# RG-LRU from its input projection on, layer 1's input normalised first, S5's powers in one tile

## The chip, the cores and the metric

The kernel runs on one core of a Trainium2 chip. The time is device time of one execution in microseconds; the time before is 1248.59 us, the median of three runs (1243.89 to 1249.86).

## The reference

Two layers of a hybrid decoder trunk on x of 512 tokens by 1024 channels, float32. Each layer computes

```
h = RMSNorm(x, ln_mix_pre);  p = h @ w_in          # columns go to four mixers of 256 channels
m = concat[GLA(p_A), DiffAttn(p_B), S5(p_C), RG-LRU(p_D)] @ w_out
x = x + RMSNorm(m, ln_mix_post)
x = x + RMSNorm(relu(RMSNorm(x, ln_ffn_pre) @ ffn_w1)**2 @ ffn_w2, ln_ffn_post)

RMSNorm(x, g) = x * rsqrt(mean(x*x) + 1e-6) * g    # per token
RG-LRU: xc = conv4(rx); r, i = sigmoid(xc @ w_a + b_a), sigmoid(xc @ w_x + b_x)
        a = exp(-8 r softplus(-lam)); h_t = a h_(t-1) + sqrt(1 - a^2) (i * xc); out = h * gelu(rg)
S5:     a complex diagonal state per group of 16 channels; its tables need the powers w^0 .. w^127
        of each state's rotation, as cosine and sine
GLA:    gate = log_sigmoid(glr @ w_gate + b_gate) / 16, glr being a projection of rank 16
```

## The kernel before

"Layer 1" is the first layer (l = 0 in the code), "layer 2" the second.

Activations lie with channels on the partitions, 512 tokens along a row. Every float32 product of a weight W and an input X is made of three matmuls on split operands: high parts h and wh, rounded to the TensorE format, and remainders l and wl (`mm3`, L294: wh h, wh l, wl h). A weight of 4x128 rows by 256 columns is loaded into one of three `raw` buffers (L256), cast to wh by ScalarE and subtracted to wl by VectorE or GpSimd (`w_part`, L245; which of the two is `E.split_eng`, where 'g' is GpSimd). For layer 2 the split weights have been stored in DRAM ahead (`early_gen`).

The instructions are written as generators. A projection yields between its pieces, and at each yield the mixers that run in the background are advanced by given rates (`advance`, L1139). The program order so made gives each instruction its priority; a scheduler then puts each engine's queue in order at build time, and each engine works through its queue in that order. `tc.high_priority(offset=O.evp)` raises an instruction's priority; the evictions of the projections' accumulators out of PSUM have it. BANKS gives projections two banks each of `pg` and three of `pd`.

Start of layer 1 (L1192 to L1239). TensorE runs WARM = 38 matmuls on zeros. x is loaded transposed (`xT`), slice by slice of 128 channels with quarters of the first four weights between them; each slice is scaled by the norm's gain alone and split into h and l (L1225). So the first projection, dqk (queries and keys of the attention, `gemm_first`, L330), starts before the norm's token scale is known. Squares of the slices are added up (`SumSq`), TensorE sums them over channels (L541), VectorE makes the reciprocal root (`rkeep`, L1239) and TensorE spreads it over the partitions (L548) into `rbc`. Every eviction of layer 1's projections then multiplies by `rbc` on VectorE (L1340, L1359, L1392), the rotary tables do so too (L1327), and the token-major ones scale on ScalarE (L1374).

All later norms work otherwise: squares with a running sum per block of 128 tokens (L1280), a root (L1260), the identity times that scale (`dg`, L1286), and `make` (L1288): TensorE multiplies x by `dg`, which transposes and scales it at once, ScalarE writes h (L1302) and VectorE l (L1303), two blocks of tokens at a time. `gemm_blocks` (L353) then runs the product for the first 256 tokens, calls the second `make`, and runs the second half.

Order of the projections in layer 1: dqk, dv, glr, gqk, gv, gog, u, rg, rx; in layer 2 the last are rx, rg. `glr_gen` (L1378) makes the gate's input of rank 16; its copy out of PSUM (L1392) has ordinary priority. `maybe_start` (L1400) starts a mixer when its inputs are projected: the attention (`diff_gen`, L1046; scores L1063, exponentials L1078, transposes L1098) after dqk and dv, S5 after u, RG-LRU after rx and rg both. S5's preparation (`s5_prep_gen`, L608) runs behind dqk in layer 1 and beside layer 1's feed-forward for layer 2; its last part makes the powers: for each half of the channels seven doublings of the tables COS and SIN, six VectorE instructions each (`cmul`, L669). `lru_gen` (L850) convolves rx (L858, L861), multiplies by the gates' weights (L867, L868), makes a and the input of the recurrence, scans (L895), and multiplies by the GELU of rg (L899, L901). The output projection (`gemm_wide`, L408) takes the mixers' results in the order GLA, attention, S5, RG-LRU.

Of the kernel before, what the change touches and what calls it, by code (L numbers as in the profile page):

```python
# [17 lines left out]
P = 128  # L18
# [94 lines left out]
def host_pack(I):  # L113
# [31 lines left out]
    return dict(xT=np.ascontiguousarray(I["x"][0].T), xt=np.ascontiguousarray(I["x"][0]),  # L145
# [25 lines left out]
def hybrid_trunk(ctx, tc, I, out, consts):  # L171
# [158 lines left out]
    def gemm_first(wids, xs, consume):  # L330

        ps = [(pd if m // 2 % 2 else pg)() for m in range(4)]
        for kh in range(2):
            W = [w_get(w[kh]) for w in wids]

            def prod(m, k):
                cs = slice(m % 2 * P, m % 2 * P + P)
                Wm, kk = W[m // 2], 4 * kh + k
                mm3(ps[m], Wm[0][:, k, cs], Wm[1][:, k, cs], xs[kk][0], xs[kk][1], kk == 0, kk == 7)

            for k in range(2 if kh else 4):
                for m in range(4):
                    prod(m, k)
                yield
            if kh:
                for m in range(4):
                    for k in (2, 3):
                        prod(m, k)
                    with tc.high_priority(offset=O.evp):
                        consume(m, ps[m])  # L350
                    yield

# [159 lines left out]

    class SumSq:

        def __init__(self, eng, tail):
            self.acc, self.eng, self.tail = None, eng, tail
            self.ends = {}

        def add(self, c, src, hf=None):
            if hf is None:
                sq = wq("sq")
                act.activation(sq, src, AF.Square)
                if c >= self.tail:
                    self.ends[c] = sq
                elif self.acc is None:
                    self.acc = sq
                else:
                    self.eng.tensor_tensor(self.acc, self.acc, sq, ALU.add)  # L530
            else:
                if c not in self.ends:
                    self.ends[c] = wq("sq")
                act.activation(self.ends[c][:, 256 * hf:256 * hf + 256], src, AF.Square)

        def tok(self, bs=range(4)):
            ps = psm()
            tl = [self.acc] + list(self.ends.values())
            for b in bs:
                for i, t in enumerate(tl):  # L540
                    pe.matmul(ps[:, b:b + 1], t[:, b * P:b * P + P], C[:, C_BO + 6:C_BO + 7],  # L541
                              start=i == 0, stop=i == len(tl) - 1)
            return ps[:, bs[0]:bs[-1] + 1]

    def bcast_tok(col, n=4):
        ps = psm()
        for b in range(n):
            pe.matmul(ps[:, b * P:b * P + P], col[:, b:b + 1].to_broadcast([P, P]), ident,  # L548
                      start=True, stop=True)
        return ps[:, 0:n * P]  # L550
# [57 lines left out]
    def s5_prep_gen(l):  # L608
# [138 lines left out]
        yield  # L747
        for h in range(2):
            js = slice(4 * h, 4 * h + 4)
            tabs = [wt(k) for k in ("COS", "SIN", "RC")]  # L750
            ct, st, rc = (t.rearrange("p (j c) -> p j c", j=4) for t in tabs)
            pool.memset(ct[:, :, 0:1], 1.0)
            pool.memset(st[:, :, 0:1], 0.0)
            for e in range(7):
                m = 1 << e
                wr, wi = (w[:, 8 * e + 8:8 * e + 16] for w in (csw, snw))
                cmul(ct[:, :, m:2 * m], st[:, :, m:2 * m], ct[:, :, 0:m], st[:, :, 0:m],
                     bc(wr, m, js), bc(wi, m, js), 4, m)
# [91 lines left out]
    def lru_gen(l, xr, gt):  # L850
# [47 lines left out]
        for a in range(2):  # L898
            act.activation(gt[a], gt[a], AF.Gelu_apprx_tanh)  # L899
# [289 lines left out]
    sync.dma_start(PV, I["cols"])  # L1189
# [14 lines left out]
    if WARM:  # L1204
# [3 lines left out]
        act.copy(small(1, "zact", 1), z[:, 0:1])  # L1208
# [3 lines left out]
    setup_exp()  # L1212
    ssq = SumSq(v, 7)
    xin = []
    for c in range(8):
        w2 = (c // 4 * 2, c // 4 * 2 + 1)
        if c % 4 == 0:
            for i in w2:
                w_raw(i)
                w_open(i)  # L1220
        xin.append(wl("x"))
        sync.dma_start(xin[c], I["xT"][c * P:c * P + P, :])
        for i in w2:
            sync.dma_start(raws[i][:, c % 4], specs[i][:, c % 4])
        XG[c] = hl(xin[c], pv("ln_mix_pre", 0, 8, c))  # L1225
        for i, e in zip(w2, (v, pool)):
            w_part(i, slice(c % 4, c % 4 + 1), e)
        if c % 4 == 3:
            for i in w2:
                del raws[i]  # L1230
    pos[:] = [4, 4]
    sync.dma_start(C, consts[:, 0:C_N])
    w_load(3 + NRAW)
    for c in range(8):
        ssq.add(c, xin[c])
    ms = small(4, "ms4")
    v.tensor_scalar(ms, ssq.tok(), 1.0 / D, EPS, ALU.mult, ALU.add)
    rtok = small(4, "rkeep")
    v.tensor_copy(rtok, rsqrt(ms, 4))  # L1239

    def post_norm(grow, g2=None):
# [3 lines left out]
        ss, sx, part = small(8, "ss"), small(8, "sx"), small(4, "part")  # L1245
        gB = [wq("gB") for _ in range(2)]
        for c in range(2):
            sync.dma_start(gB[c], grow[:, c * 512:c * 512 + 512].to_broadcast([P, 512]))

            pool.tensor_scalar(gB[c], gB[c], 32.0, None, ALU.mult)  # L1250
        F, dg = {}, {}

        def stat(b, ct, o, f=None):
            act.activation(wq("sq"), o, AF.Square, accum_out=ss[:, 4 * ct + b:4 * ct + b + 1])
            F[b, ct] = o if f is None else f
            v.tensor_tensor(F[b, ct], o, gB[ct], ALU.mult)
            if ct == 0 and b == 3:
                v.tensor_scalar(part, ss[:, 0:4], D * EPS, None, ALU.add)

        def root(a, b):  # L1260

            y, t, xh = (small(1, k) for k in ("qy", "qt", "qh"))
            act.activation(t, a, AF.Sqrt, bias=b)
            v.tensor_scalar(xh, a, b, -0.5, ALU.add, ALU.mult)
            v.reciprocal(y, t)
            v.scalar_tensor_tensor(t, y, xh, y, ALU.mult, ALU.mult)
            v.scalar_tensor_tensor(y, t, 1.5, y, ALU.add, ALU.mult)
            return y

        def finish(b):  # L1270
            sc = root(ss[:, 4 + b:5 + b], part[:, b:b + 1])
            for c in range(2):
                if g2 is None:
                    o = wp.tile([P, 4, 256], F32, tag="raw", name=nm("o"), bufs=NRAW)
# [6 lines left out]
            if g2 is None:  # L1281
                return
# [275 lines left out]
```

## Time and profile before

| | before |
|---|---|
| median of three runs | 1248.59 us (1243.89 to 1249.86) |
| profiled execution, own time | 1246.94 us |
| its span, first to last instruction | 1244.9 us |
| mean granted TensorE clock | 0.976 |
| busy, share of the span: TensorE | 1201.6 us, 97% |
| VectorE | 683.9 us, 55% |
| ScalarE | 509.2 us, 41% |
| GpSimd | 194.2 us, 16% |

PE is TensorE's matmuls, PEld its weight loads, DVE VectorE, ACT ScalarE, POOL GpSimd, SP the queue that issues the DMAs. The profile names each instruction by the line of the kernel, here L followed by its number, and by the tiles that it writes and reads (out<-in). A granted clock of 1.00 is TensorE's full speed. Idle time of an engine is put down to the instruction that released it; a matmul's end is modelled, so starts are the better numbers.

### The profile page before, as it was taken

Reading aid. Unit: us, or ns where it says so; the run is one execution under the profiler, and the core shown is the slowest. Engines: PE = TensorE matmul, PEld = TensorE weight load, DVE = VectorE, ACT = ScalarE, POOL = GpSimd, SP = SyncE. Lnnn points to the kernel's source line nnn. Section 1 sums busy time; section 2 is a strip of 40 time slices with the busy share of each in tenths; the row PEclk is TensorE's granted clock in tenths of the full one; section 3 lists DMA queues with packets and bytes.
Section 4 is the critical chain, followed back from the end, with each engine's and each line's share of the span. In section 5 each row is a group of like instructions: output and inputs, shape, how many; then the busy total and the mean of one; then the engine's idle time right before and its main releaser. Section 6 shows DMA issues by size and latency. Waiting matters only on the chain.

```text
span 1244.9 us, 17841 instructions
## 1 busy us (share of the span) xinstructions
PE 1201.6 (97%) x6684; PEld 967.6 (78%) x6684; DVE 683.9 (55%) x1605; ACT 509.2 (41%) x950; POOL 194.2 (16%) x148
## 2 busy tenths in 40 slices
PE   8988899899999999999999999999999999999997
PEld 6755566579888888888889776777988888888886
DVE  8987568578725576545474256575641131322335
ACT  5253622456735523424341356145542341332332
POOL 5321212300000001000000000010123323333330
PEclk9998889999999999999999999899999999999999
DMA  7343122456867887866754432355432333333221
GB/s 229 98 141 116 35 86 82 136 168 208 265 211 235 283 292 241 267 210 212 253 195 141 155 109 91 116 198 203 170 100 88 100 102 92 100 97 101 87 83 67
DMA packets 126037, 191.81 MB, mean 154 GB/s; under 512 B 10688, under 2 KB 65792, under 8 KB 125952
## 3 DMA queue, kind: packets, MB, share of 16 engines
q1 hardware_dynamic: 125952, 190.69, 47.4%
q8 instruction: 52, 0.85, 0.3%
q14 instruction: 33, 0.27, 0.1%
HBM read 146.35 MB, written 44.30 MB: 153 GB/s over the span
## 4 chain that ended last, share of the span: by engine, by line
PE 83%; DVE 10%; ACT 3%; DMA 1%; issue 1%; SPq 0%; DVEq 0%; ACTq 0%
PE pg L295 7%; PE pg L296 7%; PE pg L297 7%; PE pd L296 5%; PE pd L297 5%; PE pd L295 5%; PE pd L415 4%; PE pd L417 4%; PE pd L416 4%; PE pg L415 4%; PE pg L417 3%; PE pg L416 3%; PE pd L1063 2%; PE pm L415 2%; PE pm L416 2%; PE pm L417 2%
## 5 line engine op out<-in xcount | busy, mean ns | idle before, releaser
L253 ACT CAST wh<-raw 128x1024 fp32r<-128x1024 f32 (+1 forms) x160 | 157.4, 985 | 257.4 <-PE pg L416 88.2
L254 POOL TENSOR_TENSOR wl<-raw,wh 128x1024 fp32r<-128x1024 f32 (+1 forms) x69 | 156.9, 2275 | 383.3 <-ACT wh L253 380.7
L295 PE MATMUL pg<-h,wh 128*128 128x512 f32 (+1 forms) x496 | 189.4, 383 | 2.6 <-DVE glr L1392 2.5
L297 PE MATMUL pg<-h,wl 128*128 128x512 f32 (+1 forms) x496 | 188.9, 382 | 0.2 <-DVE wl L254 0.2
L296 PE MATMUL pg<-l,wh 128*128 128x512 f32 (+1 forms) x496 | 188.4, 381 | 0.5 <-DVE l L479 0.5
L254 DVE TENSOR_TENSOR wl<-raw,wh 128x1024 fp32r<-128x1024 f32 (+1 forms) x91 | 105.9, 1164 | 144.2 <-ACT wh L253 144.0
L297 PE MATMUL pd<-h,wl 128*128 128x512 f32 (+1 forms) x336 | 120.7, 360 | 0.0
L295 PE MATMUL pd<-h,wh 128*128 128x512 f32 (+1 forms) x336 | 120.6, 360 | 0.0
L296 PE MATMUL pd<-l,wh 128*128 128x512 f32 (+1 forms) x336 | 120.4, 359 | 0.0
L295 PEld LDWEIGHTS pg<-h,wh 128*128 128x128 f32 x496 | 95.7, 193 | 21.7 <-DVE glr L1392 2.9
L297 PEld LDWEIGHTS pg<-h,wl 128*128 128x128 f32 x496 | 95.7, 193 | 17.6 <-issue 1.4
L296 PEld LDWEIGHTS pg<-l,wh 128*128 128x128 f32 x496 | 95.8, 193 | 17.0 <-DVE l L479 1.2
L1474 DVE TENSOR_TENSOR s<-r 128x512 f32<-128x512 f32 x64 | 56.7, 886 | 87.4 <-ACT r L1473 87.4
L415 PE MATMUL pd<-wh,h 128*128 128x512 f32 x240 | 93.7, 390 | 0.9 <-DMA wh<-early 0.9
L417 PE MATMUL pd<-wl,h 128*128 128x512 f32 x240 | 93.6, 390 | 0.4 <-DVE wl L254 0.4
L416 PE MATMUL pd<-wh,l 128*128 128x512 f32 x240 | 93.4, 389 | 0.0
L415 PE MATMUL pg<-wh,h 128*128 128x512 f32 x208 | 81.4, 391 | 1.4 <-ACT h L475 1.4
L416 PE MATMUL pg<-wh,l 128*128 128x512 f32 x208 | 81.0, 389 | 0.0
L417 PE MATMUL pg<-wl,h 128*128 128x512 f32 x208 | 81.0, 389 | 0.0
L297 PEld LDWEIGHTS pd<-h,wl 128*128 128x128 f32 x336 | 63.6, 189 | 9.4
L295 PEld LDWEIGHTS pd<-h,wh 128*128 128x128 f32 x336 | 63.2, 189 | 9.6 <-ACT wh L253 0.3
L296 PEld LDWEIGHTS pd<-l,wh 128*128 128x128 f32 x336 | 63.5, 189 | 9.4
(421 smaller groups left out, 2162.6 us busy)
## 6 DMA issues: line engine op xcount, KB each, us to landing
raw<-in_ffn_w SPq DMA_DIRECT2D x128, 512.0 KB, 3.9
early<-eh SPq DMA_DIRECT2D x52, 256.0 KB, 3.1
early<-el SPq DMA_DIRECT2D x52, 256.0 KB, 4.1
wh<-early SPq DMA_DIRECT2D x23, 512.0 KB, 3.6
wl<-early SPq DMA_DIRECT2D x23, 512.0 KB, 4.7
ex<-in_w_in SPq DMA_DIRECT2D x36, 256.0 KB, 4.8
raw<-in_w_in SPq DMA_DIRECT2D x14, 512.0 KB, 3.7
xd<-xr SPq DMA_DIRECT2D x24, 256.0 KB, 2.9
```

Source lines behind the costliest of these rows:

```text
L253: act.copy(h[:, k], raws[i][:, k])
L254: eng.tensor_tensor(lo[:, k], raws[i][:, k], h[:, k].bitcast(F32), ALU.subtract)
L295: pe.matmul(ps, wh, xh, start=first, stop=False, **kw)
L296: pe.matmul(ps, wh, xl, start=False, stop=False, **kw)
L297: pe.matmul(ps, wl, xh, start=False, stop=last, **kw)
L415: pe.matmul(o, xs[kk][0][:, ts_], h, start=kk == 0, stop=False)
L416: pe.matmul(o, xs[kk][1][:, ts_], h, start=False, stop=False)
L417: pe.matmul(o, xs[kk][0][:, ts_], lo, start=False, stop=kk == 7)
L1063: pe.matmul(pp[c], qs[h // 2][r:r + 32, i * P:i * P + P], ks[h // 2][r:r + 32, 0:pp[c].shape[1]], start=i == blocks[0], stop=False, tile_p ...
L1474: v.tensor_tensor(s, r, r, ALU.mult)
```

## The change

Layer 1's input goes through the same norm as all others: `post_norm` is cut in two, and its second part, `pre_norm`, is used at the start with x loaded token-major. `rbc`, `SumSq`, `bcast_tok` and `gemm_first` are gone; layer 1's evictions are plain ScalarE copies as in layer 2, and dqk runs through `gemm_blocks`. The first three weights are loaded whole, split on VectorE, into other slots of SBUF. The constants are loaded second, the small columns (PV) after block 1 of x. WARM is 80. `glr`'s copy gets the evictions' priority. Layer 1 projects rx before rg; in both layers RG-LRU starts when rx is there and waits for rg only before its last step. S5's first four doublings are made in one tile for both halves, with both parts of the complex number in one instruction, and copied into the tables by ScalarE.

```diff
@@ s5_prep_gen
+        pw = wq("pw")[:, 0:256].rearrange("p (c j m) -> p c j m", c=2, j=8)
+        pool.memset(pw[:, 0, :, 0:1], 1.0)
+        pool.memset(pw[:, 1, :, 0:1], 0.0)
+        for e in range(4):
+            m = 1 << e
+            wr, wi = (w[:, 8 * e + 8:8 * e + 16] for w in (csw, snw))
+            xa, xb = (wq("cm")[:, 0:16 * m].rearrange("p (c j m) -> p c j m", c=2, j=8) for _ in range(2))
+            tt(xa, pw[:, :, :, 0:m], bc2(wr, m), ALU.mult)
+            tt(xb, pw[:, :, :, 0:m], bc2(wi, m), ALU.mult)
+            tt(pw[:, 0, :, m:2 * m], xa[:, 0], xb[:, 1], ALU.subtract)
+            tt(pw[:, 1, :, m:2 * m], xa[:, 1], xb[:, 0], ALU.add)
+            yield
         for h in range(2):
...
-            pool.memset(ct[:, :, 0:1], 1.0)
-            pool.memset(st[:, :, 0:1], 0.0)
-            for e in range(7):
+            for c, t in enumerate((ct, st)):
+                act.copy(t[:, :, 0:16], pw[:, c, js])
+            for e in range(4, 7):
...
@@ lru_gen
         for a in range(2):
+            while gt[a] is None:
+                yield
             act.activation(gt[a], gt[a], AF.Gelu_apprx_tanh)
@@ the start
-        act.copy(small(1, "zact", 1), z[:, 0:1])
+        act.activation(small(1, "zact", 1), z[:, 0:1], AF.Sqrt)
...
-        sync.dma_start(xin[c], I["xT"][c * P:c * P + P, :])
-        for i in w2:
-            sync.dma_start(raws[i][:, c % 4], specs[i][:, c % 4])
-        XG[c] = hl(xin[c], pv("ln_mix_pre", 0, 8, c))
...
-    v.tensor_copy(rtok, rsqrt(ms, 4))
+    def pre_norm(g2, keep):
+        sx, dg = small(8, "sx"), {}
+        def half(b, c):
+            act.activation(wq("sq"), X[b, c], AF.Square, accum_out=sx[:, 2 * b + c:2 * b + c + 1])
+        def done(b):
             m0 = small(1, "ms2")
             v.tensor_scalar(m0, sx[:, 2 * b:2 * b + 1], D * EPS, None, ALU.add)
             dg[b] = small(P, "dg")
...
+            if keep:
+                for e in range(2):
+                    for c in range(2):
+                        spill(b + e, c)
+        return half, done, make
+    E.split_eng = "v"
+    half, done, make = pre_norm(lambda c: pv("ln_mix_pre", 0, 8, c), False)
+    x_load(0)
+    sync.dma_start(C, consts[:, 0:C_N])
+    x_load(1)
+    sync.dma_start(PV, I["cols"])
+    home.update(enumerate((wg, wg, wb)))
+    w_load(1)
+    x_load(2)
+    x_load(3)
+    w_load(2)
+    for b in range(4):
+        for c in range(2):
+            half(b, c)
+        done(b)
+        if b == 1:
+            make(0)
+            setup_exp()
@@ ev_mul (ev_silu and ev_tok likewise)
-                if l == 0:
-                    v.tensor_tensor(o, i, r, ALU.mult)
-                else:
-                    act.copy(o, i)
+                act.copy(o, i)
@@ glr_gen
-            if l == 0:
-                v.tensor_tensor(t, ps, rbc[0:32], ALU.mult)
-            else:
+            with tc.high_priority(offset=O.evp):
                 v.tensor_copy(t, ps)
@@ maybe_start
-            if "lru" not in started and have("rx", "rg"):
+            if "lru" not in started and have("rx"):
                 started.add("lru")
+                st["rg"] = [None, None]
                 start(lru_gen(l, st["rx"], st["rg"]), O.rate["lru"])
@@ the projections
-                g = gemm_first if l == 0 else lambda *a: gemm_blocks(*a, make)
-                g = g(WID[l, "dqk"], XG, lambda m, ps: evs[m // 2](m % 2, ps))
+                g = gemm_blocks(WID[l, "dqk"], XG, lambda m, ps: evs[m // 2](m % 2, ps), make)
@@ parameters
-WARM = 38
+WARM = 80
-    dict(order=["dqk", "dv", "glr", "gqk", "gv", "gog", "u", "rg", "rx"],
+    dict(order=["dqk", "dv", "glr", "gqk", "gv", "gog", "u", "rx", "rg"],
```

## Rows read from the trace of the kernel before

**Rows 1.** By stage: window, length, PE, PEld, DVE, ACT, POOL busy, clock, DMA, GB/s.

```profile
0.00:37.00 37.00, 32.26 (x163) 25.98 (x164) 33.49 (x138) 20.05 (x39) 17.71 (x22) 0.95 0.70 216
37.00:112.00 75.00, 62.50 (x427) 47.72 (x425) 70.53 (x288) 31.35 (x87) 22.38 (x23) 0.95 0.40 126
112.00:165.00 53.00, 49.54 (x186) 30.39 (x187) 31.08 (x91) 28.34 (x61) 9.53 (x8) 0.76 0.16 51
165.00:228.00 63.00, 57.09 (x627) 42.64 (x626) 44.86 (x98) 16.35 (x24) 14.39 (x13) 0.97 0.34 100
228.00:242.00 14.00, 10.74 (x30) 5.85 (x29) 11.07 (x13) 4.64 (x8) 6.12 (x3) 0.88 0.47 165
...
284.00:640.00 356.00, 355.86 (x1753) 299.24 (x1754) 209.52 (x398) 158.00 (x260) 8.06 (x16) 1.00 0.73 237
...
700.00:850.00 150.00, 147.73 (x1080) 105.50 (x1078) 88.58 (x235) 71.67 (x168) 7.37 (x13) 0.97 0.40 137
```

**Rows 2.** TensorE's waits, 0 to 285 us: who for whom; total, times, longest.

```profile
PE pd L1098 <- ACT p L1078: 5.1, 2, 3.9
PE pd L1063 <- ACT p L1078: 4.4, 2, 2.4
PE pd L867 <- DVE xc L861: 3.3, 1, 3.3
...
PE pg L295 <- DVE glr L1392: 2.5, 1, 2.5
```

**Rows 3.** Timeline of the start, TensorE: start, duration, line, operands, idle before.

```profile
0.97 4.11 PE L1211 MATMUL pm<-zero 128*128 128x128 bf16 x38 [0.97 <-DVE zero L1207]
...
36.66 0.28 PE L391 MATMUL pg<-wh,h 128*128 128x256 f32 x1
```

**Rows 4.** Timeline at the boundary of the two layers, 640 to 652 us.

```profile
641.07 0.29 ACT L1263 ACTIVATE qt<-ss,part 128x1 f32<-128x1 f32 x1
...
642.45 1.42 DVE L1279 SCALAR_TENSOR_TENSOR xr<-f,qy,xr 128x512 f32<-128x512 f32 x2
...
642.88 1.95 PE L1298 MATMUL pg<-dg,xr 128*128 128x128 f32 x16
...
643.24 0.63 ACT L1280 ACTIVATE sq<-xr 128x512 f32<-128x512 f32 x1 [1.87 <-DVE xr L1279]
...
644.91 0.46 ACT L1302 ACTIVATE h<-pg,PV 128x256 fp32r<-128x256 f32 x1
...
645.40 0.48 DVE L1303 SCALAR_TENSOR_TENSOR l<-pg,PV,h 128x256 fp32r<-128x256 f32 x1
...
647.82 0.28 PE L295 MATMUL pd<-h,wh 128*128 128x256 f32 x1
...
647.93 0.28 PE L296 MATMUL pd<-l,wh 128*128 128x256 f32 x1
```

**Rows 5.** DMA issues, 0 to 40 us: count, size, median us to landing.

```profile
x<-in_xT SPq DMA_DIRECT2D x8, 256.0 KB, 4.0
```

**Rows 6.** Busy time of one window, behind the wait for the gate input.

```profile
59.50:63.00 3.50, 3.50 (x9) 2.78 (x10) 3.50 (x20) 2.90 (x10) 0.00 (x0) 0.52 0.22 85
```

**Rows 7.** VectorE by line and by form, two timeline rows, layer 2's ScalarE eviction.

```profile
L1340 DVE TENSOR_TENSOR u<-pg,rbc 128x512 f32<-128x512 f32 x2 | 2.2, 1105 | 1.0 <-PE pg L297 1.0
...
L1340 DVE TENSOR_TENSOR gqk<-pg,rbc 128x512 f32<-128x512 f32 x2 | 1.4, 680 | 0.0
...
L673 DVE TENSOR_TENSOR COS<-cm,cm 128x4 f32<-128x4 f32 x2 | 0.3, 155 | 0.0
...
102.00 2.41 DVE L675 TENSOR_TENSOR cm<-SIN,cs 128x64 f32<-128x64 f32 x1
...
101.86 4.81 POOL L254 TENSOR_TENSOR wl<-raw,wh 128x1024 fp32r<-128x1024 f32 x2 [3.60 <-ACT wh L253]
...
L1342 ACT COPY gqk<-pg x2: 586/586/587, 680.1 to 685.5; 128x512 f32<-128x512 f32 x2
```

**Rows 8.** TensorE's waits, 850 to 880 us (layer 2's tail).

```profile
PE pg L415 <- ACT h L475: 1.1, 1, 1.1
```

More of the change, by code (lines that the diff above doesn't have):

```diff
@@ L328, in gemm_T @@
                     yield
[L330 to L351, printed above, removed]
     def gemm_blocks(wids, xs, consume, need):
@@ L1186, in hybrid_trunk @@
                 WID[l, "f2", qd, ct] = [add_wide(I["ffn_w2"][l], 8 * qd + 2 * k2, 512 * ct) for k2 in range(4)]
-    sync.dma_start(PV, I["cols"])
     XG = [None] * 8
@@ L1231, in hybrid_trunk @@
[L1231 to L1238, printed above, removed]
-    v.tensor_copy(rtok, rsqrt(ms, 4))
[L1241 to L1274, printed above, removed]
-                    o = o.rearrange("p k c -> p (k c)")[:, 0:512]
-                    v.scalar_tensor_tensor(o, F[b, c], sc, X[b, c], ALU.mult, ALU.add)
-                    sync.dma_start(out[0, b * P:b * P + P, 512 * c:512 * c + 512], o)
-                else:
-                    v.scalar_tensor_tensor(X[b, c], F[b, c], sc, X[b, c], ALU.mult, ALU.add)
-                    act.activation(wq("sq"), X[b, c], AF.Square, accum_out=sx[:, 2 * b + c:2 * b + c + 1])
-            if g2 is None:
-                return
@@ new lines, in root @@
+    def root(a, b):
+        y, t, xh = (small(1, k) for k in ("qy", "qt", "qh"))
+        act.activation(t, a, AF.Sqrt, bias=b)
+        v.tensor_scalar(xh, a, b, -0.5, ALU.add, ALU.mult)
+        v.reciprocal(y, t)
+        v.scalar_tensor_tensor(t, y, xh, y, ALU.mult, ALU.mult)
+        v.scalar_tensor_tensor(y, t, 1.5, y, ALU.add, ALU.mult)
+        return y
+    def pre_norm(g2, keep):
[3 more added lines that the diff above has]
+        def done(b):
@@ L1313, in hybrid_trunk @@
         O.__dict__.update(LAYER[l])
-        if l == 0:
-            E.split_eng = O.mix
         E.mix = {}
         st = {}
-        rbc = None
-        if l == 0:
-            rbc = cp.tile([P, T], F32, name="rbc")
-            act.copy(rbc, bcast_tok(rtok))
         st["cosr"], st["sinr"] = wb("cosr"), wb("sinr")
@@ L1357, in f @@
                 t = wg(key)
-                if l == 0:
-                    v.tensor_tensor(t, ps, rbc, ALU.mult)
-                act.activation(t, t if l == 0 else ps, AF.Silu)
+                act.activation(t, ps, AF.Silu)
                 st[key][m] = t
@@ L1369, in f @@
             def f(b, n, ps):
-                if l > 0:
-                    act.copy(tl[b // 2], ps)
-                    return
-                for i in range(n):
-                    act.activation(st[key][b + i], ps[:, 256 * i:256 * i + 256], AF.Copy,
-                                   scale=rtok[:, b + i:b + i + 1])
+                act.copy(tl[b // 2], ps)
             return f
```

100 lines of the change are left out of this document (39 added, 61 removed).

## The prediction, made before the result was known

> **What bounds the kernel now.** I first read the busy times by stage [rows 1]. From 284 to 640 us TensorE is busy for 355.86 of 356 us at granted clock 1.00: feed-forward stages have nothing to give. Layer 2's mixers, 700 to 850 us, lose 2.27 us and run at 0.97. The first 242 us are different: TensorE is busy for 212.1 of them, so 29.9 us are idle, and the clock falls to 0.95, 0.76 and 0.88 in the stretches where it idles. VectorE is busy 70.53 of 75 us from 37 to 112 us, so there it is the engine that TensorE waits behind. The waits of TensorE [rows 2] name the places: transposes and score products of the difference attention behind the exponentials of ScalarE (5.1 and 4.4 us, themselves behind VectorE's maxima), the RG-LRU's gate products behind its convolution (3.3 us), the first product after the gate input (`glr`, 2.5 us). Then I read the start on TensorE [rows 3]: warm-up from 0.97 us, and the projection behind the first one (dv) at 36.66. An idle time costs twice: behind the 2.5 us at `glr` the granted clock is 0.52 for 3.5 us [rows 6], about the lower of its two levels, 1.2 GHz.
>
> So the change matters only in layer 1's mixers and at layer 2's RG-LRU; everything else must shift as a block.
>
> **The change part by part.** Each term is against the profiled execution (span 1244.9, own time 1246.94 us); the median shown is 1248.59, 1.65 above, and I add that at the end.
>
> *The start.* Before, projections began on unnormalised x and a token scale (rbc) was multiplied in afterwards. Now x is normalised first: per block of 128 tokens two squares, a root, a scaled identity; then `make` (32 records a pair of blocks) writes the transposed, scaled h and l. Every step of this stands at the layer boundary [rows 4]: a square 0.63 us, the root from its Sqrt at 641.07 to its first use at 642.45, 1.4 us, 16 of make's records 1.95 us, then 0.46 us on ScalarE and 0.48 on VectorE for each of eight slices. x's block 1 is the fifth transfer on SP's queue; at the queue's pitch of 0.43 us from 0.72 it is issued at 2.4 and, at 4.0 us to landing [rows 5], there at 6.4. Two squares 1.3, root 1.4: the scale stands at 9.1. Half of make 1.95, first slice 0.94: the first product can start near 12.0; weights 0 and 1, seventh and eighth on the queue, are issued at 3.3 and 3.7, have landed by 8 and are split meanwhile. The warm-up grows from 38 to 80 matmuls; at 4.11 us for 38 that ends near 9.6, under the wait for x, so it costs nothing (0.5 us if x came sooner). From 12.0 the product is 192 matmuls of 256 columns at the 0.12 us pitch (647.82, 647.93) [rows 4], 23.0 us, and the second make inside it 3.5: 38.5. Three raw buffers mean that weight 3 is only issued after weight 0 is split, near 12.5; landing 4.0 and a split of four 256-column pieces, 4 x 0.46 on ScalarE and the last 0.48 on VectorE, bring it to 18.8; TensorE wants it after the first 48 matmuls, at 17.8: +1.0. So dv starts at 39.5 where it started at 36.66: **+2.8 us**. Bounds: 0, if the steps up to 12.0 overlap by that much; +9.8, if the first product, and then weight 3, each stand one landing of 4.0 longer, the second in place of the 1.0. I take the worked value, which is the rows' own.
>
> *The copy of the gate input.* It gets the priority of the other evictions, so it is not behind S5's preparation on VectorE any more. The 2.5 us wait [rows 2] goes, and with it the slow stretch: 3.5 us at 0.52 is 3.5 x 0.48 = 1.7 lost. **-4.2 us**. Between nothing (the wait moves to the next bank) and -4.2; one wait with one cause, so the full value.
>
> *Less work on VectorE.* The rbc multiplies go: gqk 2 x 0.68 and the sine table, as large, 0.7 in the saturated stretch, gog and u (2 x 1.1 us) later [rows 7]. The evictions become ScalarE copies of 0.59 us, as layer 2 has them; ScalarE is busy 31 of 75 us there, which hides them. If that cover were gone, eight copies would be 4.7 us. S5's powers: per half of the channels the first four doublings were 24 small instructions, 48 together, now 16 over both halves, and four copies on ScalarE. At 0.155 us for the smallest [rows 7], 48 are 7.4; the 16 new ones run from 8 to 128 elements (between 0.155 and the 0.68 of 512), by my estimate 3.3: 4.1 saved. Together 6.2 us; VectorE's queue starts 2.8 later, so what stands behind it is 3.4 earlier: **-3.4 us**. Bounds: 0, if the chain of the attention and not VectorE's queue sets the pace; -13, if both waits on the exponentials (9.5 us) and a slow stretch like [rows 6] twice went. In layer 2's preparation, beside the feed-forward, the same saving is worth nothing [rows 1]; the initial Sqrt, the constants' new place on the queue and the missing write-back of x cost nothing either, under the wait for x.
>
> Against this stands one row: an instruction of 128x64 elements took 2.41 us at 102.00, over twice what u's 128x512 takes [rows 7], while GpSimd split weights from 101.86 on; the longest wait on the exponentials, 3.9 us [rows 2], comes after it. The Trainium skill, SBUF — State Buffer, "Who interferes with whom", says that a VectorE instruction with two SBUF inputs and a GpSimd one that reads SBUF shut each other out for the whole instruction; the trace agrees. By that rule cutting small instructions does not shorten such a stall: the next two-input instruction meets the split instead, the term would be near 0 and the sum 1241 us; with none there at that moment it would be rival B.
>
> *RG-LRU.* Its input projection now comes before the gate's, and the mixer starts as soon as that is there; the gate is awaited only at the end. Before, TensorE stood 3.3 us at 236.5 for the convolution [rows 2], and 228 to 242 us ran at 0.88, 14 x 0.12 = 1.7 lost [rows 1]. The gate projection, 48 matmuls of 512 columns at twice the pitch of 256, 11.5 us, now lies behind the convolution and covers it: **-5.0 us**; 0 if S5 is last in its place. In layer 2, with the order as it was, only the earlier start acts; its wait for the RG-LRU's output is 1.1 us [rows 8]: **-1.0 us**.
>
> Sum: 2.8 - 4.2 - 3.4 - 5.0 - 1.0 = -10.8. 1246.9 - 10.8 = 1236.1; on the scale of the median **1238 us**.
>
> **Rivals.**
> *A: the start eats the gain.* x, constants and weights share one queue, and the first product needs all of block 0 and 1. For it: before, the first product needed one slice of x. Against: 12 us of make and squares fit between the landings. Start +9.8 and no relief on VectorE: 1238 + 7.0 + 3.4 = 1248 us.
> *B: the attention recovers.* 112 to 165 us ran at 0.76: 12.7 us lost to the clock. If the stall at 102 meets nothing that TensorE waits for, the 3.9 us wait goes, and with it a third of the lost clock, 4.2: another -8, 1230 us. For: layer 2 does the same mixers at 0.97. Against: there are other GpSimd splits.
> *C: slower.* ScalarE becomes the place where projections stick. Eight evictions now stand in its queue, in order, with exponentials that wait for VectorE. Where one is held for over 2.1 us with both banks of the projection full, TensorE stands as it stood for `glr`. Held 3 us each, 8 x 3 = 24 - 10.8 = +13: 1262 us; it decides over (10.8 + 6.2) / 8 = 2.1 us each. For: that is what happened at `glr`, on VectorE. Against: layer 2 evicts in this way and idles 2.3 us in 150 [rows 1].
> *D: the RG-LRU's wait only changes owner.* S5's scans use VectorE at the same time, and what the convolution takes they give; the tail's 5 us stay: 1243 us.
>
> **How the numbers follow.** Forecast 0.42 (own range 1231 to 1244), A 0.18, B 0.20, C 0.10, D 0.10. A measurement tells 0.5%, 6.2 us, from no change: faster is under 1242.3, slower over 1254.8. Faster: 0.38 of the forecast, B 0.20, D 0.05: 0.63. Same: 0.04 + 0.17 + 0.05 = 0.26. Slower: C and 0.01 of A: 0.11. The range runs from B with the relief at its bound, 1222, to 1252, which leaves out C.
>
> **What would show it.** First 256-column product near 12 us and dv near 39.5; no wait of TensorE behind `glr` and the clock at 1.00 after it; S5's powers done some 3 us earlier; no wait of the RG-LRU's gate products, and the feed-forward of layer 1 begun near 274 instead of 284; layer 2's mixers 1 us shorter. The prediction is wrong if dv starts after 43, if ScalarE's evictions appear as TensorE's longest releaser, or if 112 to 165 us keeps its clock of 0.76 and its waits in full.

## The result and the profile after

The changed kernel takes 1228.29 us (median of 4 runs, 1226.16 to 1229.13) where the kernel before, on the same chip, takes 1246.24: a ratio of 0.9868, 95% interval 0.9832 to 0.9903, or 18 us faster. The forecast was 1238, with 1222 to 1252 as its range: the direction is right, and the gain is 7 us larger than the sum forecast. The time lies below the forecast's own range (1231 to 1244) and next to rival B's 1230. The profiled execution has a span of 1226.1 us where before had 1244.9, 18.8 less, so it is a fair picture of the difference.

Where the 18.8 us went shows at three landmarks, the first transposing product (`make`) at each normalisation. Layer 1's feed-forward begins at 262.5 us where it began at 282.2 before, 19.7 earlier; layer 2's input is normalised from 624.2 (642.9 before), and layer 2's feed-forward begins at 859.9 (879.2). All of the gain is made ahead of layer 1's feed-forward. Layer 2's mixers, from landmark to landmark, take 235.7 us for 236.3; the seven kernels run here with this same layer 2 lie between 232.9 and 236.3, so its forecast microsecond can't be read here. In the answer for the line of `make` the columns are its count, its shortest, median and longest duration in ns, and its first and last start:

```profile
L1203 PE MATMUL pg<-dg,xr x16: 270/275/377, 262.5 to 265.0; 128*128 128x128 f32 x16
```

The busy times by stage, in the columns of [rows 1]:

```profile
0.00:39.00 39.00, 37.86 (x338) 37.50 (x339) 30.89 (x121) 21.36 (x49) 5.88 (x13) 1.00 0.68 221
39.00:112.00 73.00, 62.35 (x429) 48.22 (x428) 64.21 (x294) 32.70 (x88) 21.50 (x19) 0.93 0.40 125
112.00:165.00 53.00, 51.59 (x334) 33.69 (x335) 31.62 (x105) 31.61 (x70) 12.01 (x10) 0.97 0.22 69
165.00:200.00 35.00, 33.22 (x353) 25.58 (x349) 26.51 (x50) 9.79 (x13) 7.69 (x10) 1.00 0.33 96
200.00:214.00 14.00, 12.02 (x123) 6.78 (x121) 9.89 (x23) 5.40 (x8) 3.96 (x1) 0.88 0.64 209
...
681.00:831.00 150.00, 144.58 (x1073) 102.54 (x1072) 90.56 (x239) 71.97 (x169) 6.86 (x13) 0.98 0.37 123
```

The stretch from 112 to 165 us is the one to see. It ran at a granted clock of 0.76 before [rows 1]; now it runs at 0.97. Before it lost 3.5 us idle and 49.54 x 0.24 = 11.9 to the clock; now 1.4 and 51.59 x 0.03 = 1.5. That is 12.4 us. From 39 to 112 us nothing improved: TensorE idles 10.7 us where it idled 12.5 from 37 to 112, and the clock is 0.93 for 0.95. From 39 us to the landmark, one row for the kernel before and one for the changed one:

```profile
39.00:282.00 243.00, 216.28 (x1414) 154.88 (x1414) 182.74 (x534) 106.99 (x226) 53.32 (x47) 0.92 0.35 109
```

```profile
39.00:262.00 223.00, 206.60 (x1432) 151.55 (x1431) 166.26 (x527) 118.08 (x244) 53.51 (x44) 0.96 0.37 117
```

Of the 20 us between them 10.3 are idle time of TensorE (26.7 to 16.4) and 9.7 its busy time, which the higher clock shortens.

TensorE's waits up to 285 us, longest sums first, to be set against [rows 2]:

```profile
PE ps L659 <- ACT bx L653: 4.1, 1, 4.1
PE pg L295 <- DVE glr L1338: 3.0, 1, 3.0
PE pd L1055 <- ACT p L1035: 2.0, 2, 1.2
PE pd L822 <- DVE xc L816: 2.0, 1, 2.0
```

The waits for the exponentials (`p`) fell from 9.5 us (5.1 and 4.4) to 2.0. The wait behind the gate input's copy (`glr`), which was to go, is 3.0 where it was 2.5. The RG-LRU's (`xc`) fell from 3.3 to 2.0. S5's `bx` is new; it is ScalarE's copy of `bd`, which VectorE makes, and no eviction of a projection. From 62.4 to 66.0 us, behind the copy of `glr`, the clock is 1.00 as forecast, but TensorE is busy for only 1.66 of the 3.6 us before it waits again.

S5's powers were to be done some 3 us earlier. Their last instruction, in the kernel before and in the changed one:

```profile
110.57 0.42 DVE L676 TENSOR_TENSOR SIN<-cm,cm 128x256 f32<-128x256 f32 x1
```

```profile
93.39 0.41 DVE L614 TENSOR_TENSOR SIN<-cm,cm 128x256 f32<-128x256 f32 x1
```

That is 17 us earlier.

The start came out as forecast, TensorE's timeline says:

```profile
0.97 7.13 PE L1167 MATMUL pm<-zero 128*128 128x128 bf16 x80 [0.97 <-DVE zero L1163]
7.93 0.66 PE L1203 MATMUL pg<-dg,x 128*128 128x128 f32 x4
...
11.76 0.36 PE L295 MATMUL pd<-h,wh 128*128 128x256 f32 x1
...
39.03 0.28 PE L368 MATMUL pg<-wh,h 128*128 128x256 f32 x1
```

The first product starts at 11.76 (forecast 12.0), dv at 39.03 (39.5) where it started at 36.66 [rows 3].

### The profile page after: what moved, and what is told of

Read it like the earlier page. It is cut to its first block, busy times and chain, and to the rows that moved or that the text cites. A ratio compares the mean times of both kernels' runs of the same rounds, so it can differ in the third digit from the quotient of the medians.

```text
span 1226.1 us, 18116 instructions
## 1 busy us (share of the span) xinstructions
PE 1194.3 (97%) x6862; PEld 973.8 (79%) x6862; DVE 657.9 (54%) x1543; ACT 519.6 (42%) x977; POOL 180.9 (15%) x134
## 4 chain that ended last, share of the span: by engine, by line
PE 81%; DVE 4%; ACT 3%; issue 3%; DMA 2%; POOL 0%; DVEq 0%; SPq 0%; ACTq 0%; POOLq 0%
PE pg L295 7%; PE pg L297 7%; PE pg L296 7%; PE pd L295 5%; PE pd L296 5%; PE pd L297 5%; PE pd L392 4%; PE pd L394 4%; PE pd L393 4%; PE pg L392 4%; PE pg L393 4%; PE pg L394 4%; PE pm L392 2%; PE pm L393 2%; PE pm L394 2%
## 5 line engine op out<-in xcount | busy, mean ns | idle before, releaser
L253 ACT CAST wh<-raw 128x1024 fp32r<-128x1024 f32 x145 | 151.9, 1049 | 262.4 <-PE pg L393 88.7
L254 POOL TENSOR_TENSOR wl<-raw,wh 128x1024 fp32r<-128x1024 f32 x59 | 143.9, 2440 | 390.4 <-ACT wh L253 381.4
L254 DVE TENSOR_TENSOR wl<-raw,wh 128x1024 fp32r<-128x1024 f32 x86 | 106.3, 1236 | 145.9 <-ACT wh L253 140.3
L295 PE MATMUL pd<-h,wh 128*128 128x512 f32 (+1 forms) x352 | 123.8, 352 | 0.0
L296 PE MATMUL pd<-l,wh 128*128 128x512 f32 (+1 forms) x352 | 123.5, 351 | 0.1
L297 PE MATMUL pd<-h,wl 128*128 128x512 f32 (+1 forms) x352 | 123.5, 351 | 0.0
L296 PEld LDWEIGHTS pd<-l,wh 128*128 128x128 f32 x352 | 66.5, 189 | 9.0 <-DVE l L1208 0.4
L297 PEld LDWEIGHTS pd<-h,wl 128*128 128x128 f32 x352 | 66.5, 189 | 8.8
L295 PEld LDWEIGHTS pd<-h,wh 128*128 128x128 f32 x352 | 66.5, 189 | 8.8
```

The lines of the kernel that those rows point to most:

```text
L253: act.copy(h[:, k], raws[i][:, k])
L254: eng.tensor_tensor(lo[:, k], raws[i][:, k], h[:, k].bitcast(F32), ALU.subtract)
L295: pe.matmul(ps, wh, xh, start=first, stop=False, **kw)
L296: pe.matmul(ps, wh, xl, start=False, stop=False, **kw)
L297: pe.matmul(ps, wl, xh, start=False, stop=last, **kw)
```

## What holds VectorE, by rows of the changed kernel

Two waits that the change was meant to remove are still there, and behind both stands one kind of row. First the `glr` wait: VectorE, then GpSimd, then TensorE.

```profile
50.33 0.29 DVE L610 TENSOR_TENSOR cm<-bc,nai 128x128 f32<-128x128 f32 x1
50.53 2.39 DVE L595 TENSOR_TENSOR cr<-cr,den 128x8 f32<-128x8 f32 x1
52.84 0.15 DVE L597 TENSOR_TENSOR t<-nr,PV 128x8 f32<-128x8 f32 x1
52.92 2.47 DVE L611 TENSOR_TENSOR cd<-cm,cm 128x128 f32<-128x128 f32 x1
...
61.69 0.67 DVE L1338 COPY glr<-pg 32x512 f32<-32x512 f32 x1
...
50.36 4.88 POOL L254 TENSOR_TENSOR wl<-raw,wh 128x1024 fp32r<-128x1024 f32 x2 [7.67 <-DVE cm L609]
...
54.03 0.39 PE L1335 MATMUL pg<-l,wz 128*32 128x512 f32 x1
62.42 0.50 PE L295 MATMUL pg<-h,wh 128*128 128x512 f32 x1 [3.03 <-DVE glr L1338]
```

An instruction of 8 elements takes 2.39 us where its neighbour of the same shape takes 0.15, and one of 128 takes 2.47 where its neighbour takes 0.29; both lie inside GpSimd's two weight splits, 50.36 to 55.24. So VectorE comes to the copy of `glr` at 61.69, although the product was done at 54.42. The two holds put its queue back by 4.4 us (2.24 and 2.18 over the neighbours); other instructions ahead of the copy in that queue take the rest. The RG-LRU's wait is the same story:

```profile
201.71 2.80 DVE L816 SCALAR_TENSOR_TENSOR xc<-rx,PV,xc 128x511 f32<-128x511 f32 x1
...
204.57 0.74 DVE L816 SCALAR_TENSOR_TENSOR xc<-rx,PV,xc 128x510 f32<-128x510 f32 x1
...
199.72 4.24 POOL L254 TENSOR_TENSOR wl<-raw,wh 128x1024 fp32r<-128x1024 f32 x1 [4.28 <-ACT wh L253]
...
206.84 1.34 PE L822 MATMUL pd<-xc,wlru 128*128 128x512 f32 x2 [1.98 <-DVE xc L816]
```

One of the convolution's instructions takes 2.80 us, its sister 0.74: 2.06 more, and TensorE waits 1.98. The Trainium skill, SBUF — State Buffer, "Who interferes with whom", says that a VectorE instruction with two SBUF inputs contends with a GpSimd one that reads SBUF, and that of the two the one issued later is blocked for the whole of the other. The first held row agrees: 2.39 us, against 4.88 for GpSimd's two splits, 2.44 each. So does what is not held, in this pair of splits:

```profile
105.45 4.72 POOL L254 TENSOR_TENSOR wl<-raw,wh 128x1024 fp32r<-128x1024 f32 x2 [13.33 <-ACT wh L253]
106.08 0.20 DVE L881 RECIPROCAL drd<-sum 128x8 f32<-128x8 f32 x1 [1.77 <-ACT p L1035]
106.31 1.54 DVE L882 TENSOR_TENSOR dr<-drd 128x8 f32<-128x8 f32 x1
108.38 1.80 DVE L1050 SCALAR_TENSOR_TENSOR cc<-cc,lamv,sum 128x1 f32<-128x1 f32 x1
```

The RECIPROCAL, which has one input, takes 0.20 us inside the first split; the two-input instruction behind it takes 1.54 us, until that split ends, and the next one 1.80 us, until the second ends. One input is not always safe: in the kernel before a TENSOR_SCALAR with one tile as input took 2.40 us at 48.07, inside a split. And the split at 199.72 takes 4.24 us itself: in its first 1.9 us VectorE's two-input instructions run back to back, so there GpSimd seems to be the one that is held.

I counted VectorE's instructions of at most 512 elements that took over 1.6 us, from 36 us to the landmark of layer 1's feed-forward. The kernel before has 12, the changed one 9; shorter holds, like the 1.54 above, are not in the count. From 36 us on both kernels have sixteen whole splits on GpSimd, so it is not their number that changed but what they meet. The experiments start from this.

## Experiments

Each run is timed beside the kernel before, on the same chip, and told by its ratio to it. "FFN 1" is the landmark of layer 1's feed-forward in the run's own profile; "held" is the count just described. A landmark comes from one execution, and that execution lay up to 5.3 us off its kernel's median (a_noprio 1225.15 for 1230.48, a_lruold 1227.49 for 1232.59, a_mixv 1217.01 for 1213.85, b_mixv 1214.57 for 1210.59).

| kernel | median us | ratio to before | 95% interval | FFN 1 at | held |
|---|---|---|---|---|---|
| before | 1244.2 to 1246.3 | 1 | | 282.2 | 12 |
| changed | 1228.29 | 0.9868 | 0.9832 to 0.9903 | 262.5 | 9 |
| a_again | 1230.23 | 0.9881 | 0.9852 to 0.9909 | 263.0 | 9 |
| a_noprio | 1230.48 | 0.9874 | 0.9840 to 0.9908 | 262.2 | 10 |
| a_lruold | 1232.59 | 0.9906 | 0.9873 to 0.9939 | 263.1 | 11 |
| a_s5old | 1232.39 | 0.9890 | 0.9855 to 0.9926 | 266.6 | 10 |
| a_startonly | 1238.97 | 0.9955 | 0.9932 to 0.9978 | 276.3 | 13 |
| a_ones | 1230.96 | 0.9880 | 0.9854 to 0.9906 | 265.5 | 12 |
| a_glract | 1228.75 | 0.9858 | 0.9829 to 0.9887 | 263.2 | 9 |
| a_mixv | 1213.85 | 0.9748 | 0.9720 to 0.9776 | 250.5 | 2 |
| b_mixv | 1210.59 | 0.9712 | 0.9684 to 0.9741 | 250.1 | 3 |
| b_s5 | 1239.52 | 0.9943 | 0.9918 to 0.9968 | 280.5 | 12 |
| b_lru | 1246.68 | 0.9993 | 0.9972 to 1.0015 | 275.7 | 15 |
| a_best | 1206.06 | 0.9669 | 0.9644 to 0.9693 | 243.8 | 0 |

### One part undone at a time

**a_again**: the changed kernel, unedited.

> The changed kernel once more, unedited, on the chip of the three runs beside it. Its profiled execution shows how far the landmarks move with nothing edited: if they are the program's, layer 1's feed-forward (first make) starts within 1 us of 262.5; if they are an execution's, several us off. Median expected 1228 to 1230.

Measured: 263.0 at the landmark, the same longest waits to 0.1 us, ratio 0.9881. So the shape of layer 1 belongs to the program, and the landmarks of these two executions differ by half a microsecond.

**a_noprio**

```
-            with tc.high_priority(offset=O.evp):
-                v.tensor_copy(t, ps)
+            v.tensor_copy(t, ps)
```

> The changed kernel, with the copy of the gate input (glr) back at the priority of the code around it. Theory 1 (the raised priority moves nothing, because VectorE is behind its plan there: the copy ran only at 61.7 us, 7 us after its product, and TensorE stood 3.0 us): within 2 us of the changed kernel, 1228, and the wait behind glr as long as before, 2 to 4 us. Rival (the priority is worth its forecast 4.2 us and the 3.0 us are a different wait): about 1232, with the wait behind glr over 5 us.

Measured: no difference (0.9874 for a_again's 0.9881), the wait behind `glr` 3.2 us. Theory 1 holds; the priority is worth nothing that shows here.

**a_lruold**

```
-    dict(order=[..., "u", "rx", "rg"],        # layer 1
+    dict(order=[..., "u", "rg", "rx"],
-            if "lru" not in started and have("rx"):
+            if "lru" not in started and have("rx", "rg"):
-                st["rg"] = [None, None]
```

> The changed kernel, with layer 1's order back to rg, rx and the RG-LRU mixer started in both layers only when both projections are there. Theory 1 (the forecast's term, partly: the changed kernel still waits 2.0 us for the convolution where the kernel before waited 3.3): about 3 to 4 us longer, 1231 to 1232, with the wait of the gate products back near 3.3 us. Forecast: 6 us longer, 1234. Rival (the wait only changes owner): within 1 us of 1228.

Measured: 0.9906, about 3 us over a_again, with the intervals overlapping, so the size is not settled. The convolution's wait went to 2.6 us, not to 3.3, and a wait of 1.4 us for `gry` is new. In layer 2 the wait moved. TensorE's wait for the RG-LRU's last output, in the changed kernel and then in this one:

```profile
PE pg L392 <- ACT h L452: 3.2, 1, 3.2
```

```profile
PE pg L392 <- ACT h L452: 1.1, 1, 1.1
```

With the early start this wait is 2.1 us longer, where the forecast had it 1.0 shorter. The reason that I give in b_lru's expectation, the second gate's Gelu in ScalarE's tail, doesn't stand: in the changed kernel that Gelu runs at 830.02, behind the `h` that ends the wait (827.60), and this `h` waited for VectorE's `o`. The early start brings that `h` 5.4 us earlier (833.00 in this run) and TensorE to the place 7.5 us earlier (825.09 for 832.56); why TensorE comes earlier stays open. In the time the 2.1 us don't show: later in the output projection this run waits 1.1 us for a weight's DMA, which the changed kernel doesn't, and layer 2's mixers take 235.1 us for 235.7.

**a_s5old**: the block that builds `pw` replaced by the 84 instructions of before.

```
-        pw = wq("pw")[:, 0:256].rearrange("p (c j m) -> p c j m", c=2, j=8)
...
-            for e in range(4, 7):
+            for e in range(7):
```

> The changed kernel, with S5's powers built half by half in 84 instructions as before. Theory 1 (VectorE's queue paces the attention, and its lead is what lifts the stretch that ran at 0.76): 4 us more on VectorE and with it back to a slower clock there, 4 to 9 us longer, 1232 to 1237, with VectorE busy some 4 us more. Rival (what matters is which instruction meets a GpSimd split, not how much VectorE has to do): within 2 us of 1228, or shorter, with the work on VectorE more all the same.

Measured: 0.9890, no difference that the intervals show; the landmark is 3.6 to 4.1 us later and the stretch from 112 to 165 us runs at 0.93. The powers end at 110.11 us, as late as in the kernel before. The landmark speaks for theory 1, the medians don't decide.

**a_startonly**: the three edits above together.

> The changed kernel with the three edits above undone together: what is left of the change is the normalisation first, with the token scale's multiplies gone and layer 1's evictions on ScalarE. If the parts add: 1228 + 0 + 3.5 + 6 = about 1238, still 8 us below the kernel before, although the start itself costs 2.4 us; then the evictions' move from VectorE to ScalarE is the main part. Rival (the removed multiplies are worth little, as forecast: 2 of 3.4 us): 1246 or more, no better than the kernel before.

Measured: 1238.97, as theory 1 gave, and the interval lies below 1. The normalisation first, with the evictions on ScalarE, gains 5.6 us though dv still starts 2.2 us later than before (38.87). The three parts undone singly move the landmark by -0.8, +0.1 and +3.6 us from a_again's, together by +13.3, but two of those three executions lay 5 us below their medians. By the medians it is 0.3, 2.4 and 2.2 us singly and 8.7 together, each with 3 to 4 us of interval either way: whether the parts add is not settled, and theory 1's hit doesn't show that they do.

**a_ones**

```
+        if l == 0:
+            one = cp.tile([P, T], F32, name="one")
+            pool.memset(one, 1.0)
...
-                act.copy(o, i)
+                if l == 0:
+                    r = one.rearrange("p (t s) -> p s t", s=4) if key == "u" else one
+                    v.tensor_tensor(o, i, r, ALU.mult)
```

> The changed kernel with layer 1's evictions of gqk, gog, u, rx and rg back on VectorE, as multiplications by a tile of ones (the arithmetic of the token scale, without the scale; gog gets its Silu behind it, as before). Theory 1 (the move of the evictions to ScalarE is what took load off VectorE, the larger part of what the start-only kernel gains): VectorE some 8 us busier before 265 us, layer 1's feed-forward 3 to 8 us later, 1232 to 1237. Rival (ScalarE and VectorE are as good a place, and the gain is the shift of everything behind the start): within 2 us of 1228.

Measured: 0.9880 for a_again's 0.9881, although VectorE is busy 670.8 us where it was busy 657.5. The ten multiplications are 7.6 us of the 13; what the rest is I did not trace, but three more instructions are held. The rival holds by the medians: this cost nothing that they show, to some 4 us (the landmark is 2.5 us later). The edit also takes eight copies off ScalarE, so it shows, within that interval, that one engine is as good a place for these evictions as the other. It speaks against the forecast's pricing of the removed multiplies by their durations.

**a_glract**

```
-                v.tensor_copy(t, ps)
+                act.copy(t, ps)
```

> The changed kernel with the gate input's copy on ScalarE instead of VectorE. Theory 1 (TensorE stands 3.0 us there because VectorE is late, and the next wait, 4.1 us for S5's bx, is what VectorE's lateness costs next): the 3.0 us wait goes, and the wait behind bx grows by part of it; 0 to 3 us shorter, 1225 to 1228. Rival (the wait is a clean stall): 3 us off and nothing in its place, 1225, with the wait for bx at 4.1 or less.

Measured: no difference that shows (0.9858), and neither theory: the wait behind `glr` stays at 3.2 us. ScalarE's timeline says why:

```profile
60.98 0.71 ACT L639 COPY CA<-cd 64x256 f32<-64x256 f32 x2 [3.29 <-DVE cd L611]
61.71 0.29 ACT L636 COPY ca<-bc 64x128 f32<-64x128 f32 x1
61.91 0.40 ACT L639 COPY CA<-cd 64x256 f32<-64x256 f32 x1
62.33 0.57 ACT L1338 COPY glr<-pg 32x512 f32<-32x512 f32 x1
```

ScalarE idles 3.29 us for VectorE's `cd` (L611, a line of S5's preparation; one instruction of it was held for 2.47 us in the changed kernel), and the copy stands behind the copies of `cd` in its queue. VectorE, which was held here for 2.40 and 2.35 us at 50.98 and 53.50, makes ScalarE's queue late too; moving this one instruction to the other engine didn't go round it.

### The splits off GpSimd

**a_mixv**: fourteen of layer 1's weight splits go to VectorE; three of the output projection's stay on GpSimd (the expectation says 16).

```
-         mix='g', out='gggv', ff='v', ...        # layer 1
+         mix='v', out='gggv', ff='v', ...
```

> The changed kernel with layer 1's mixer-stage weight splits all on VectorE instead of GpSimd. In the trace of the changed kernel a VectorE instruction of 128x8 elements took 2.39 us and one of 128x128 2.47 us while GpSimd's two splits ran from 50.36 for 4.88 us. Theory 1 (a GpSimd split holds VectorE for its own 2.4 us; on VectorE the same split costs 1.24 us): 16 splits, some 1 us less of VectorE's time each, no VectorE instruction of under 128x512 elements above 1 us any more, 3 to 8 us shorter: 1220 to 1225. Rival (GpSimd's splits cost VectorE only where they meet a two-input instruction, and VectorE pays 16 x 1.24 = 20 us more): longer, 1233 to 1245.

Measured: 1213.85, 16 us below a_again and more than theory 1 gave; the intervals are apart. The two middle stages, and the copy of `glr`:

```profile
39.00:112.00 73.00, 71.22 (x484) 55.95 (x482) 62.71 (x315) 40.47 (x93) 5.55 (x15) 1.00 0.46 144
112.00:165.00 53.00, 51.69 (x417) 35.00 (x416) 41.67 (x132) 27.16 (x70) 2.64 (x7) 0.97 0.25 73
```

```profile
56.19 0.67 DVE L1338 COPY glr<-pg 32x512 f32<-32x512 f32 x1
```

From 39 to 112 us TensorE is busy 71.22 of 73 us at clock 1.00, where the changed kernel had 62.35 at 0.93, and VectorE is busy 62.71 us for 64.21 though it now does these splits itself. The copy of `glr` comes 5.5 us earlier, 0.7 us behind its last product, with no wait of TensorE behind it. What remains of the largest waits:

```profile
PE pm L393 <- DVE l L453: 2.2, 1, 2.2
PE pd L1020 <- ACT p L1035: 2.1, 2, 1.1
```

**b_mixv**: the same edit on the kernel before. Eight quarter pieces in the first projection and three of the output projection's splits stay on GpSimd (the expectation says none).

> The kernel before with one edit: layer 1's weight splits up to the output projection all on VectorE, none on GpSimd. Open is how much of the change's 18 us came from fewer small VectorE instructions being held by GpSimd splits (12 of them over 1.6 us in the trace before, 9 after, 2 in the run of the changed kernel without GpSimd splits). Theory 1 (the collisions are the main loss of the kernel before too, and the change took part of it back): 12 to 20 us faster than before, 1225 to 1232, with the stretch that ran at 0.76 back at 0.95 or more; the change on top of it (the run of the changed kernel without GpSimd splits, 1214) is then worth 11 to 18. Rival (collisions mattered only because of the change's new order): within 5 us of 1245; the start's 13 splits on VectorE would even cost.

Measured: 1210.59, 36 us faster than before, well under theory 1's 1225. The stretch from 112 to 165 us misses theory 1's 0.95: it runs at 0.90, so GpSimd's splits are not all that slowed it. Its stages and its longest wait:

```profile
37.00:112.00 75.00, 73.66 (x489) 55.02 (x487) 71.55 (x324) 40.64 (x101) 6.33 (x18) 1.00 0.46 141
112.00:165.00 53.00, 50.83 (x365) 35.44 (x365) 40.29 (x134) 24.03 (x56) 2.12 (x6) 0.90 0.26 79
```

```profile
PE pd L867 <- DVE xc L861: 3.1, 1, 3.1
```

This is the run that says most about what the change's gain is. Without these splits on GpSimd the kernel before stands at 0.9712 and the changed one at 0.9748: a ratio of 1.0037, and with the half-widths of about 0.0028 each put together as 0.0040, between no difference and 0.8% slower. The expected 11 to 18 us on top are excluded. VectorE is busy 71.55 of 75 us, more than the 70.53 by which I read it as the engine that TensorE waits behind [rows 1], and TensorE idles 1.3 us there: a full VectorE was not the bound.

A second reading of this pair is not excluded. From 39 to 250 us TensorE is busy 202.5 of 211 us in a_mixv and 201.7 in b_mixv, so without the splits there is little idle time left for the change's edits to win, whatever they were worth with the splits in place. Either way the change's gain and that of moving the splits are not two gains that add.

One forecast step does show here in the waits: with the old order the RG-LRU's wait is 3.1 us without any held instruction of the convolution, and in a_mixv, with the new order, 0.4.

**b_s5** (the block of `pw` put into the kernel before) and **b_lru** (rx before rg, the early start and the later wait for the gate put into it):

> The kernel before with S5's powers built in one tile for both halves, and nothing else. The forecast gives this part 4.1 us of VectorE's time earlier; undone in the changed kernel it cost 2.2 us by the medians and 4.1 us at layer 1's feed-forward. Theory 1 (parts add): 2 to 5 us below before, 1240 to 1243. Rival (its worth hangs on which instruction meets which split): anywhere within 4 us either side of before, with the count of held instructions, not VectorE's busy time, going with it.

> The kernel before with rx before rg in layer 1 and the RG-LRU started in both layers as soon as rx is there, and nothing else. Forecast: 5.0 us in layer 1 and 1.0 in layer 2 off, 1239. Theory 1 (by the changed kernel: layer 1 gains, and layer 2 pays, because the second gate's Gelu now stands in ScalarE's tail and TensorE waits 3.2 us for the output where it waited 1.1): 4 to 5 us off at layer 1's feed-forward, 2 us lost in layer 2, about 1242. Rival (the wait changes owner): no change at layer 1's feed-forward, 1245 to 1247.

Measured: b_s5 0.9943, 7 us faster, 2 more than theory 1's bound, and with 12 held instructions as before: the rival's count does not go with the time, so where they fall must matter, or S5's saving is larger than its durations; which of the two is open. For the second speaks that the powers end at 97.88 us, 13 us earlier than before; the new block also yields ten times where the old one yielded fourteen times, which may put S5's preparation ahead in the program order. b_lru 0.9993, no change: its interval leaves at most 3.5 of the forecast's 6.0 us. Its landmark lies 6.5 us earlier, but the profiled execution (1242.78) is 4 us below the runs' median, so the landmark can't be taken at its value. By the time the rival holds: the convolution's wait is gone from the list, and S5's products wait 3.6 us for `X` where they waited 1.4. Layer 2's tail waits 3.2 us here too.

**a_best**

```
-         mix='g', out='gggv', ff='v', ...        # layer 1
+         mix='v', out='v', ff='v', ...
-            if "lru" not in started and have("rx"):
+            if "lru" not in started and have("rx", *["rg"] * l):
-                st["rg"] = [None, None]
+                st.setdefault("rg", [None, None])
```

> The changed kernel with layer 1's weight splits on VectorE up to the first feed-forward (mixers and output projection), and in layer 2 the RG-LRU started when both projections are there, as before the change. Theory 1 (the 2.2 us wait of the output projection comes from an instruction held for 2.42 us by a GpSimd split, and layer 2's tail wait falls from 3.2 to 1.1 us): 2 to 4 us below the run with the mixers' splits alone on VectorE, 1210 to 1212. Rival (both waits are replaced by others): 1213 to 1215.

Measured: 1206.06, 40 us under the kernel before (ratio 0.9669) and 8 under a_mixv, twice the gain expected and with intervals apart. The edit has two parts, which no run separates, and the kernel before was not run with them, so this doesn't say what the change adds. No instruction is held in layer 1's mixers, and layer 1's feed-forward begins 6.7 us earlier than in a_mixv. TensorE's longest waits up to 285 us, and the one at layer 2's tail:

```profile
PE pd L1020 <- ACT p L1035: 2.1, 2, 1.1
PE pg L1203 <- DVE dg L1191: 1.1, 1, 1.1
...
PE pg L392 <- ACT h L452: 1.1, 1, 1.1
```

## Why the prediction was right, and where not

*The start* (+2.8): right. dv starts 2.4 us later, and the first product came out to 0.3 us, in part by luck: the warm-up ended at 8.1 us, not 9.6, `make` began at 7.93 where the scale was forecast for 9.1, and from there to the first product it took 3.8 us where the working had 2.9.

*The copy of the gate input* (-4.2): failed. The step said the copy was "not behind S5's preparation on VectorE any more"; it is, because the order of VectorE's queue is fixed beforehand and VectorE, put back 4.4 us by two splits, comes to it 7 us after the product. I had written the stall at 102 us down as something against the VectorE term and not looked for its like ahead of `glr`, where it was too: GpSimd's splits run from 47.98 to 52.79 in the trace before, and instructions of 64 elements take 2.40 us at 48.07 and 2.38 at 50.47.

*Less work on VectorE* (-3.4): the direction is right, the measure wrong. It was priced by the durations of removed instructions; 7.6 us of such multiplications put back (a_ones) cost nothing that shows. And "there it is the engine that TensorE waits behind" read a busy share as a bound: in b_mixv VectorE is as busy and TensorE hardly waits. What came back is rival B's place: the stretch from 112 to 165 us, with 12.4 us less idle and slow time there where B had put 8. Before, the splits at 101.86 held two instructions of S5's preparation, and TensorE waited 3.9 us for the exponentials behind them [rows 2, 7]. In the changed kernel the two splits come at 105.45, when S5's powers are long done; they hold other instructions, for 1.54 and 1.80 us, and TensorE's wait at 111.11 is 0.94 us. That the later gain in the clock follows from this one displacement was argued from two traces, and b_s5 speaks against it: there the wait in this place is 1.26 us, at 108.46, and the stretch still loses 8.3 us idle and 3.6 to the clock (busy 44.72 us at 0.92). The run for it would move that pair of splits alone, and it wasn't made. In a_startonly that stretch is busy 47.31 us at 0.87: 5.7 idle and 6.2 to the clock, so 11.8 lost, still near the 15.4 of before.

*RG-LRU* (-5.0 and -1.0): too large together, and not settled how much of it is left in layer 1. The trace shows the wait 1.3 us shorter; the 1.98 us left are no more than the 2.06 that one held instruction costs. Alone on the kernel before the two steps move the time by nothing that shows, at most 3.5 us. In layer 2 the wait grew by 2.1 us instead of going, though layer 2's length doesn't show it.

*Rivals*: A (the start eats the gain) and C (evictions stuck on ScalarE) did not come. ScalarE's `bx`, a 4.1 us wait, is near to C's kind, though neither an eviction nor behind exponentials; it is gone from the longest waits of a_mixv. B's number came, and its place, on top of the forecast, but not shown to be by its cause. D (the RG-LRU's wait changes owner) is what b_lru shows on the kernel before.

So the sum was right in sign, and in size partly by luck: of its four gains the `glr` term failed, the RG-LRU's two are at most 3.5 of 6.0 us on the kernel before, and what made up for them is the stretch that the prediction had priced under rival B. The likeliest reason is one that the prediction held as a side case: the change moved VectorE's work against GpSimd's splits. The two kernels without those splits show that its edits, taken together, add nothing measurable once the splits are gone; that they gained by missing splits, and not by filling idle time that the splits had made, is argued.

What stays open: a_mixv takes away VectorE's being held and also halves the time of a split (2.44 us on GpSimd, 1.24 on VectorE). The projections' products in a_mixv's profile wait 0.2 us in all for a split of VectorE, and none is listed for a split in the changed kernel, which speaks for the first, but no run separates the two. Nor does any run tell the edits' missing of splits from the ceiling named under b_mixv. Nor do I know what a_startonly's 5.6 us are made of.

## What to carry to other kernels

Before pricing an edit by the durations of the instructions it removes, look in the saturated engine's timeline for small instructions that last as long as a neighbour engine's large ones; here taking GpSimd's splits off gained 36 us, twice what the change did. A busy share of 94% names the engine that is late and not why: test it by taking the suspected cause out of both kernels, before and after, since an edit that only shuffles work past a collision can look like a gain of its own. And a raised priority did nothing here for an instruction whose queue was already late for another reason.

## What the runs showed of the hardware that was not expected

A weight split of 128x1024 on VectorE took 1.24 us, and on GpSimd 2.44 us, during which a VectorE instruction with two inputs, even one of 8 elements, took until the split's end (2.39 us), while a RECIPROCAL with one input took 0.20 us. In a_mixv, with fourteen of them moved to VectorE, TensorE was 8.9 us busier from 39 to 112 us and its granted clock there 1.00 instead of 0.93, at no rise in VectorE's busy time.
